# Branch B's output product: two plain tiles, then two tiles as one seven-block product, in turn

## The chip, the core and the metric

The kernel runs on one core of one Trainium2 chip, as one program. The metric is device time in microseconds. The kernel before takes 1298.48 us (median of 3 runs, 1298.05 to 1299.4). A change of this kernel is called faster or slower here when the medians differ by more than 0.2%, which is 2.6 us.

## The reference, cut to what matters

One inference step of a one-layer encoder over 576 frames (512 of a new stream, 64 of a running one), `D_MODEL = 1024`, all in float32:

```python
x = x + 0.5 * swiglu_ffn(rms_norm(x, ffn1_norm), ffn1_w_gate_up, ffn1_w_down)
h = rms_norm(x, mix_norm)
p = h @ w_in                       # seven parts of 1024 columns
...                                # branch A: a short convolution
y_a = (a_b * a_conv) @ w_a_out
...                                # branch B: a convolution of 31 taps
b_act = silu(layer_norm(b_conv + conv_b_bias, conv_b_ln_g, conv_b_ln_b))
y_b = b_act @ w_b_out
merged = sigmoid(gate_a) * y_a + sigmoid(gate_b) * y_b
x = x + merged @ w_out
x = x + 0.5 * swiglu_ffn(rms_norm(x, ffn2_norm), ffn2_w_gate_up, ffn2_w_down)
```

A final RMSNorm gives the outputs, beside the new histories of both convolutions. The change is about `b_act @ w_b_out`, a product of 576 x 1024 by 1024 x 1024.

## The kernel before

**Layout.** Features lie on the 128 partitions, frames along the free axis. An activation is eight tiles of 128 x 576 (`T = 576`, `KT = 8`), and a tile has two halves of 288 frames (`H`). The residual is the tiles `x0` to `x7` (`X[j]`), which live in on-chip memory through the whole program.

**A plain product.** Each operand is kept as a high and a low part (`hi` rounded to the matmul's input type, `lo` what is left). An output tile takes 8 steps over the contraction x 2 halves x 3 parts (hi·hi, hi·lo, lo·hi) = 48 matmuls of 128 x 288 (`mm`), into the two banks of one accumulator buffer `mm_n`. There are four such buffers, taken in turn.

**A block product.** Both feed-forward parts already compute a pair of output tiles by Winograd's form of Strassen's product: seven blocks instead of eight, each 4 contraction steps x 3 parts = 12 matmuls into one bank (`block`, `Forms`, `plan_block`). A pair takes 84 matmuls in place of 96. It needs sums of the weights (four additions of 128 x 512 tiles), sums of the activations (`combine`: four half-tile operations on each pair of tiles, then their high and low parts), and VectorE steps that put the seven results together.

**Weights.** `Stream` takes weights through three steps per unit of 128 x 512. SyncE issues the load of a `raw` tile from HBM (six raw buffers, L228, in strict order). ScalarE writes the high part and its negative (`begin`). Then GpSimd issues a DMA that adds the raw tile to the negative and so leaves the low part; for sums of weights VectorE subtracts instead. A raw buffer is free once that DMA has landed. `lead` keeps six units done ahead of the unit that TensorE multiplies, and each engine runs its instructions in the order in which the program emits them.

**Around the change.** The last two stages of the mixer go as follows. Eight plain products `p6` give gate B (`gb_of`), while `work` holds the steps of branch B's normalisation and swish, which make the operand tiles `BA[0..7]`. Then eight plain products `yb` by `w_b_out`: after each, VectorE multiplies by the gate, adds to `M[j]` (branch A's share) and, with ScalarE, splits the sum into `MS[j]`, 3.05 us of work in a chain. Then eight products `o` by `w_out`, contraction over `MS[0..7]`, whose results are added to `X[j]`. `M` had buffers of its own, four in the pool `act` and four in the pool `w`.

## Time and profile before

| | |
|---|---|
| median of 3 runs | 1298.48 us (1298.05 to 1299.4) |
| the profiled execution, device time | 1297.62 us |
| its span in the profile | 1295.8 us, so 1.82 us lie around it |
| TensorE busy | 1283.5 us, 99% of the span |
| VectorE busy | 897.0 us, 69% |
| ScalarE busy | 763.7 us, 59% |
| granted TensorE clock over the run | 0.997 |

In the profiled execution the eight `p6` products run from 748.1 to 798.0 us, the eight `yb` products to 847.9, and the `o` products follow. All of VectorE's, ScalarE's and GpSimd's instructions carry line 83 (the recording helper), so rows are told apart by their tiles. A row of the timeline gives start, duration, engine, operation and, in brackets, how long the engine sat idle before it and what ended that. Times in the windows view are busy microseconds of each engine in a stretch; its "DMA share" is how busy the core's 16 DMA engines were on average.

### The profile page before, as it was taken

How to read it: one execution, taken by the hardware profiler on the slowest of the kernel's cores; microseconds unless marked ns; L12 is line 12 of the kernel's file. 1: busy time of each engine (PE TensorE's matmuls, PEld its weight loads, DVE VectorE, ACT ScalarE, POOL GpSimd, SP SyncE). 2: the span in 40 equal slices, each digit the busy share in tenths (PEclk: the TensorE clock that was granted, in tenths of full speed). 3: DMA queues.
4: the chain of work that ended last, by engine and by line, in shares of the span. 5: the costliest groups of instructions: out<-in, count | busy, mean ns of one | idle time of the engine just before them, and what ended most of it. 6: DMA issues, size and time to landing. Idle time of an engine off the chain costs nothing.

```text
span 1295.8 us, 25664 instructions
## 1 busy us (share of the span) xinstructions
PE 1283.5 (99%) x9754; PEld 1281.9 (99%) x9754; DVE 897.0 (69%) x1480; ACT 763.7 (59%) x1351; POOL 372.0 (29%) x470
## 2 busy tenths in 40 slices
PE   9999999999999999999999999999999999999996
PEld 9999999999999999999999999999999999999996
DVE  6868668648846998898884160336867858847955
ACT  7655646546776655555544674467665656654664
POOL 0032332232333444333321322222242242241230
PEclk9999999999999999999999999999999999999998
DMA  7286786886798898877885977776697696796782
GB/s 215 74 180 153 164 179 153 175 181 151 151 194 185 168 206 175 169 168 169 178 170 117 211 158 164 169 154 139 145 179 171 145 199 149 161 206 140 159 176 80
DMA packets 285931, 213.15 MB, mean 164 GB/s; under 512 B 15344, under 2 KB 248816, under 8 KB 285808
## 3 DMA queue, kind: packets, MB, share of 16 engines
q0 software_dynamic: 57600, 95.05, 44.9%
q1 hardware_dynamic: 226336, 115.49, 31.4%
q8 instruction: 77, 1.26, 0.4%
q10 hardware_dynamic: 1872, 0.97, 0.3%
q14 instruction: 46, 0.38, 0.1%
HBM read 113.81 MB, written 2.62 MB: 90 GB/s over the span
## 4 chain that ended last, share of the span: by engine, by line
PE 96%; DVE 2%; ACT 1%; DMA 1%; issue 0%; DVEq 0%; SPq 0%; ACTq 0%
PE mm L83 96%; DVE acc L83 0%; DMA raw<-in_ffn_w_gate_up_dram 0%; ACT tmp L83 0%; DVE tmp L83 0%; DVE g L83 0%; DVE act L83 0%; DMA gains<-in_params_dram 0%; ACT act L83 0%; DVE x L83 0%; ACT g L83 0%; DVEq L1254 0%; DVE r L83 0%; ACT r L83 0%; ACT acc L83 0%
## 5 line engine op out<-in xcount | busy, mean ns | idle before, releaser
L83 PE MATMUL mm<-act,u 128*128 128x288 f32 x4686 | 659.8, 293 | 0.0
L83 PEld LDWEIGHTS mm<-act,u 128*128 128x128 f32 x4686 | 630.5, 188 | 0.0
L83 PE MATMUL mm<-act,g 128*128 128x288 f32 x2778 | 398.8, 294 | 0.1
L83 PEld LDWEIGHTS mm<-act,g 128*128 128x128 f32 x2778 | 377.5, 188 | 0.3 <-DVE tmp L83 0.3
L83 PE MATMUL mm<-act,act 128*128 128x288 f32 (+2 forms) x2244 | 306.1, 293 | 0.0
L83 PEld LDWEIGHTS mm<-act,act 128*128 128x128 f32 x2244 | 297.3, 188 | 0.0
L83 POOL DMA_DIRECT2D u<-raw x197 | 172.5, 876 | 409.9 <-ACT u L83 298.2
L83 ACT CAST u<-raw 128x512 fp32r<-128x512 f32 (+2 forms) x203 | 116.2, 572 | 156.1 <-PE mm L83 119.1
L83 POOL DMA_DIRECT2D g<-raw x117 | 102.3, 874 | 272.9 <-ACT g L83 212.7
L83 DVE SCALAR_TENSOR_TENSOR w<-g,prm,w 128x606 f32<-128x606 f32 x232 | 179.2, 842 | 1.4 <-ACT w L83 1.4
L83 DVE TENSOR_TENSOR tmp<-mm,tmp 128x288 f32<-128x288 f32 (+1 forms) x239 | 107.6, 458 | 67.8 <-PE mm L83 50.9
L83 POOL DMA_DIRECT2D act<-raw x86 | 74.7, 869 | 196.1 <-ACT act L83 187.7
L83 ACT ACTIVATE u<-u 128x512 fp32r<-128x512 f32 (+2 forms) x197 | 116.9, 593 | 6.2
L83 ACT CAST g<-raw 128x512 fp32r<-128x512 f32 (+2 forms) x126 | 69.0, 548 | 39.1 <-DMA raw<-in_ffn_w_down_dram 15.8
L83 DVE SCALAR_TENSOR_TENSOR tmp<-mm,r 128x576 f32<-128x576 f32 x48 | 36.3, 757 | 71.8 <-PE mm L83 71.8
L83 ACT CAST u<-w 128x512 fp32r<-128x512 f32 x79 | 48.9, 619 | 60.1 <-DVE w L83 52.8
L83 ACT CAST g<-w 128x512 fp32r<-128x512 f32 x77 | 47.7, 619 | 60.1 <-DVE w L83 51.5
L83 ACT CAST act<-tmp 128x576 fp32r<-128x576 f32 x84 | 56.7, 675 | 42.7 <-DVE tmp L83 41.1
L83 DVE TENSOR_TENSOR act<-tmp,act 128x576 fp32r<-128x576 f32 x84 | 62.1, 755 | 18.2 <-ACT act L83 16.5
L83 ACT ACTIVATE g<-g 128x512 fp32r<-128x512 f32 (+2 forms) x117 | 66.4, 568 | 3.7
L83 ACT CAST act<-raw 128x512 fp32r<-128x512 f32 (+3 forms) x94 | 55.6, 592 | 14.5 <-PE mm L83 6.6
L83 DVE TENSOR_TENSOR w<-raw,raw 128x512 f32<-128x512 f32 x78 | 53.4, 685 | 12.8 <-DMA raw<-in_ffn_w_gate_up_dram 12.8
(88 smaller groups left out, 808.6 us busy)
## 6 DMA issues: line engine op xcount, KB each, us to landing
raw<-in_ffn_w_gate_up_dram SPq DMA_DIRECT2D x171, 256.0 KB, 3.4
u<-raw POOLq DMA_DIRECT2D x140, 256.0 KB, 4.1
raw<-in_w_in_dram SPq DMA_DIRECT2D x112, 256.0 KB, 3.6
act<-raw POOLq DMA_DIRECT2D x80, 256.0 KB, 4.0
raw<-in_ffn_w_down_dram SPq DMA_DIRECT2D x96, 192.0 KB, 3.8
g<-raw POOLq DMA_DIRECT2D x60, 256.0 KB, 3.9
g<-raw POOLq DMA_DIRECT2D x43, 192.0 KB, 4.5
u<-raw POOLq DMA_DIRECT2D x41, 192.0 KB, 4.5
```

The costliest lines, as they stand in the source:

```text
L83: return self.tc.keep_in_program_order(fn(*args, **kwargs))
```

## The change

Of the eight `yb` tiles, tiles 0, 1, 4 and 5 stay plain products. Tiles 2 and 3, and tiles 6 and 7, become one block product each. In the program's order: plain 0, plain 1, block pair (2, 3), plain 4, plain 5, block pair (6, 7). What belongs to it:

- The block product's activation sums are formed from branch B's swish tiles: two of the four `combine`/`split` steps inside `work` during `p6`, two after the last `p6` product.
- The weights of a pair are loaded as four `raw` tiles with every second row block (`step=2`), and the units' pools are chosen by hand (`homes_b`, `few`). During `p6` four units are kept ready instead of six (`ws.ahead = 4`), and six again from `yb` on.
- `M` is now `X` itself: the residual is stored to DRAM (`kept0` to `kept7`, eight stores of 288 KB) after the first feed-forward part, branch A's share is written over it, and it is loaded back (eight loads of 288 KB, `back`) once `MS[j]` has been made. Both kinds go on SyncE's queue, among the weight loads: as built, `kept0` to `kept7` stand between the last loads of the first feed-forward part's `w_down` and the tenth load of `w_in`, each behind the last update of its `X[j]`.
- `o`'s weight units now lie in the pools `g` and `u` rather than `act` and `u`.

```diff
     for j in range(KT):
         for b, of in ((1, c_of), (2, cv_of), (0, b_of)):
             product(("p", b, j), xg, of(j))
-
-    M, SGB, BA = [], [], []
+        nc.sync.dma_start(kept[j], X[j])
+
+    M, SGB, BA = X, [], []
...
+        if i in (3, 5):
+            work.append(lambda p=(i - 3) // 2: forms.combine(p))
+        if i in (4, 6):
+            work.append(lambda p=(i - 4) // 2: forms.split(p))
+    ws.ahead = 4
...
+    for p in range(KU // 2, KU):
+        forms.combine(p)
     take()
-    MS = []
-    for j in range(KT):
-        ps = product(("yb", j), BA)
-        dve.tensor_tensor(halves(SGB[j]), ps, halves(SGB[j]), op=ALU.mult)
-        dve.tensor_tensor(M[j], M[j], SGB[j], op=ALU.add)
-        MS.append(split(M[j]))
+    for p in range(KU // 2, KU):
+        forms.split(p)
...
+    ws.ahead = AHEAD_UNITS
+    bs = forms.operands(BA[::2] + BA[1::2])
+    def merged(j, c):
+        dve.tensor_tensor(M[j], M[j], c, op=ALU.add)
+        if j < 4:
+            MS[j] = split(M[j])
+    def plain_pair(i):
+        for j in (2 * i, 2 * i + 1):
+            ps = product(("yb", j), BA)
+            dve.tensor_tensor(halves(SGB[j]), ps, halves(SGB[j]), op=ALU.mult)
+            merged(j, SGB[j])
+    def block_pair(i):
...
+        def second():
+            dve.tensor_tensor(u3, q[3], u2, op=ALU.add)
+            dve.tensor_tensor(half(c2, 1), u3, q[2], op=ALU.subtract)
+            if i == KU - 1:
+                MS[4], MS[5] = split(M[4]), split(M[5])
+        def first():
+            dve.tensor_tensor(half(c1, 1), q[5], u4, op=ALU.add)
+            dve.tensor_tensor(c1, c1, SGB[j], op=ALU.mult)
+            merged(j, c1)
...
+        for n, xs in enumerate(bs):
+            q.append(block(ws.get(plan["yb", "s", i][n]), xs))
+            if n > 0:
+                steps[n - 1]()
+        dve.tensor_tensor(half(c2, 0), q[6], u3, op=ALU.add)
+        dve.tensor_tensor(c2, c2, SGB[j + 1], op=ALU.mult)
+        merged(j + 1, c2)
+    plain_pair(0)
+    block_pair(1)
+    back(0, 1)
+    plain_pair(2)
+    back(2, 3)
+    block_pair(3)
+    MS[6], MS[7] = split(M[6]), split(M[7])
+    back(4, 5)
...
         ps = product(("o", j), MS)
+        if n == 0:
+            back(6, 7)
```

How the instructions stand now, at the three places that matter. First VectorE from the gating of `yb` tile 1 on. Before (`mm_n` are the accumulators, `w`/`g` the gate tiles, `act` the halves of the split):

```order
L83 TENSOR_TENSOR w_1585_9774<-mm_1645_10198,w_1585_9774 128x576
L83 TENSOR_TENSOR act_1440_8744<-act_1440_8744,w_1585_9774 128x576
L83 TENSOR_TENSOR act_1653_10265<-act_1440_8744,act_1652_10263 128x576
L83 TENSOR_TENSOR g_1599_9857<-mm_1654_10267,g_1599_9857 128x576
L83 TENSOR_TENSOR act_1458_8892<-act_1458_8892,g_1599_9857 128x576
```

and in the changed kernel (`mm_1678` and `mm_1685` hold results q0, q1 and q2, q3 of the first block pair, `mm_1693` q4, q5; `w_1689` is the first weight sum of the second pair, `tmp_1671`, `tmp_1672` and `tmp_1670` are the steps that join the blocks):

```order
L85 TENSOR_TENSOR x1_91<-x1_91,w_1572_9771 128x576
L85 TENSOR_TENSOR act_1668_10324<-x1_91,act_1667_10322 128x576
L85 TENSOR_TENSOR g_1666_10294<-w_1662_10262,g_1665_10293 128x512
L85 TENSOR_TENSOR tmp_1671_10328<-mm_1678_10342,tmp_1671_10328 128x288
L85 TENSOR_TENSOR tmp_1672_10329<-mm_1685_10382,tmp_1671_10328 128x288
L85 TENSOR_TENSOR w_1689_10416<-raw_1676_10338,raw_1677_10340 128x512
L85 TENSOR_TENSOR tmp_1672_10329<-mm_1685_10382,tmp_1671_10328 128x288
L85 TENSOR_TENSOR tmp_1670_10327<-tmp_1672_10329,mm_1685_10382 128x288
L85 TENSOR_TENSOR w_1694_10440<-w_1689_10416,raw_1681_10360 128x512
L85 TENSOR_TENSOR tmp_1669_10326<-mm_1693_10425,tmp_1671_10328 128x288
L85 TENSOR_TENSOR tmp_1669_10326<-mm_1693_10425,tmp_1672_10329 128x288
L85 TENSOR_TENSOR tmp_1669_10326<-tmp_1669_10326,g_1589_9859 128x576
```

Each plain tile was three operations on VectorE. Now the joining steps of the first pair stand in one row with the weight sums of the second, and `w_1689`, which reads two raw tiles, stands ahead of everything that reads q3 to q6.

Second, SyncE's queue. Before, at the tail of `w_b_out`:

```order
L228 DMA raw_1630_10068<-in_w_b_out_dram 128x4x128
L228 DMA raw_1633_10099<-in_w_b_out_dram 128x4x128
L228 DMA raw_1639_10135<-in_w_b_out_dram 128x4x128
L228 DMA raw_1642_10166<-in_w_b_out_dram 128x4x128
L228 DMA raw_1648_10204<-in_w_b_out_dram 128x4x128
L228 DMA raw_1651_10235<-in_w_b_out_dram 128x4x128
```

and now (`raw_1650` and `raw_1675` are the weights of tile 5; `raw_1676`, `raw_1677`, `raw_1681` and `raw_1684` those of the second pair, the first two of which are added in `w_1689`):

```order
L233 DMA raw_1650_10188<-in_w_b_out_dram 128x4x128
L233 DMA raw_1675_10336<-in_w_b_out_dram 128x4x128
L1163 DMA x0_90<-kept0_6553 128x576
L233 DMA raw_1676_10338<-in_w_b_out_dram 128x4x128
L1163 DMA x1_91<-kept1_6554 128x576
L233 DMA raw_1677_10340<-in_w_b_out_dram 128x4x128
L233 DMA raw_1681_10360<-in_w_b_out_dram 128x4x128
L233 DMA raw_1684_10380<-in_w_b_out_dram 128x4x128
L233 DMA raw_1688_10401<-in_w_out_dram 128x4x128
L233 DMA raw_1692_10423<-in_w_out_dram 128x4x128
L1163 DMA x2_92<-kept2_6555 128x576
L1163 DMA x3_93<-kept3_6556 128x576
```

The reloads of `x0` to `x3` stand between the weight loads, each of them behind the split of the tile that it overwrites.

Third, VectorE at the seam between `yb` and `o`. Before (tile 6's split, tile 7, the first result of `o`):

```order
L83 TENSOR_TENSOR g_1634_10125<-mm_1690_10543,g_1634_10125 128x576
L83 TENSOR_TENSOR w_1538_9467<-w_1538_9467,g_1634_10125 128x576
L83 TENSOR_TENSOR act_1698_10610<-w_1538_9467,act_1697_10608 128x576
L83 TENSOR_TENSOR g_1635_10127<-mm_1699_10612,g_1635_10127 128x576
L83 TENSOR_TENSOR w_1547_9534<-w_1547_9534,g_1635_10127 128x576
L83 TENSOR_TENSOR act_1707_10679<-w_1547_9534,act_1706_10677 128x576
L83 TENSOR_TENSOR x0_88<-mm_1710_10684,x0_88 128x576
```

and now (`x4` to `x7` are the merged tiles 4 to 7, `mm_1740` holds q4 and q5, `mm_1751` q6 of the second pair, `mm_1759` is the first `o` product):

```order
L85 TENSOR_TENSOR act_1742_10733<-x4_94,act_1741_10731 128x576
L85 TENSOR_TENSOR act_1744_10737<-x5_95,act_1743_10735 128x576
L85 TENSOR_TENSOR tmp_1717_10619<-mm_1740_10716,tmp_1719_10621 128x288
L85 TENSOR_TENSOR tmp_1717_10619<-mm_1740_10716,tmp_1720_10622 128x288
L85 TENSOR_TENSOR tmp_1717_10619<-tmp_1717_10619,g_1633_10151 128x576
L85 TENSOR_TENSOR x6_96<-x6_96,tmp_1717_10619 128x576
L85 TENSOR_TENSOR tmp_1718_10620<-mm_1751_10766,tmp_1720_10622 128x288
L85 TENSOR_TENSOR tmp_1718_10620<-tmp_1718_10620,g_1642_10173 128x576
L85 TENSOR_TENSOR x7_97<-x7_97,tmp_1718_10620 128x576
L85 TENSOR_TENSOR act_1753_10787<-x6_96,act_1752_10785 128x576
L85 TENSOR_TENSOR act_1755_10791<-x7_97,act_1754_10789 128x576
L85 TENSOR_TENSOR x0_90<-mm_1759_10799,x0_90 128x576
```

The splits of tiles 4 and 5 and both tiles of the pair now end close together, with four splits in place of one between the last blocks and the first result of `o`.

More of the change, by code (lines that the diff above doesn't have):

```diff
@@ L1 @@
+from collections.abc import Iterator
 from contextlib import ExitStack
+from itertools import cycle
 import concourse.bass as bass
@@ L204, in __init__, with raw @@
             self.sums, self.eager = {}, False
-        def raw(self, w, row0, k, col0):
-            ap = w[0, row0 : row0 + k * P, col0 : col0 + P].rearrange("(k p) n -> p k n", p=P)
-            self.raws.append((ap, k))
+        def raw(self, w, row0, k, col0, step=1):
+            rows = w[0, row0 : row0 + k * P] if step == 1 else w[0]
+            ap = rows[:, col0 : col0 + P].rearrange("(k a p) n -> a p k n", a=step, p=P)
+            self.raws.append((ap[row0 // P if step > 1 else 0], k))
             self.last.append({})
@@ L316, in plan_tile @@
             r = ws.raw(w, row0, k, col0)
-            plan[name].append(ws.unit(r, k, home_of or home(other), low))
+            to = next(home_of) if isinstance(home_of, Iterator) else home_of or home(other)
+            plan[name].append(ws.unit(r, k, to, low))
             row0 += k * P
@@ L386, in tile_encoder_step @@
         plan_mixer(("ya", j), w_a_out, j * P)
+    few = cycle(("u", "u", "u", "act"))
     for j in range(KT):
-        plan_mixer(("p", 6, j), w_in, 6 * D + j * P)
-    for j in range(KT):
-        plan_mixer(("yb", j), w_b_out, j * P)
+        plan_mixer(("p", 6, j), w_in, 6 * D + j * P, few)
+    homes_b = iter((
+        "u", "act", "u", "act", "u", "act", "u", "act", "u", "g", "act",
+        "u", "act", "u", "g", "u", "act", "u", "g", "u", "act", "g",
+    ))
+    for i in range(KU):
+        pair = 2 * i, 2 * i + 1
+        if i % 2 == 0:
+            for j in pair:
+                plan_mixer(("yb", j), w_b_out, j * P, homes_b)
+        else:
+            plan_block(("yb", "s", i), [
+                ws.raw(w_b_out, h * P, KU, j * P, 2) for j in pair[::-1] for h in range(2)
+            ], [next(homes_b) for _ in range(7)])
     for j in IN_TURN:
-        plan_mixer(("o", j), w_out, j * P)
+        plan_tile(("o", j), w_out, 0, (KU, KU), j * P, "g")
     plan_ffn("f2", ffn2_gu, ffn2_dn)
@@ L1022, in b_of @@
         return then
+    kept = [
+        dram.tile([P, T], F32, tag=f"kept{j}", name=f"kept{j}") for j in range(KT)
+    ]
     for j in range(KT):
@@ L1051, in swish @@
             BA[j] = (BA[j], low(sig[j], BA[j]))
+            forms.b.setdefault(j // 2, []).append(sig[j])
     def ga_of(j):
@@ L1060, in then @@
         def then(ps):
[L1061 to L1063 removed]
+            dve.tensor_tensor(halves(M[j]), ps, halves(gates.pop(j)), op=ALU.mult)
         return then
@@ L1103, in tile_encoder_step @@
         advance()
-    work.extend((lambda i=i: swish(i, RL)) for i in range(KT + 2))
+    for i in range(KT + 2):
+        work.append(lambda i=i: swish(i, RL))
+        if i in (3, 5):
[3 more added lines that the diff above has]
+    ws.ahead = 4
     def gb_of(j):
@@ L1118, in tile_encoder_step, with back @@
         work.pop(0)()
+    for p in range(KU // 2, KU):
+        forms.combine(p)
     take()
-    MS = []
-    for j in range(KT):
-        ps = product(("yb", j), BA)
-        dve.tensor_tensor(halves(SGB[j]), ps, halves(SGB[j]), op=ALU.mult)
-        dve.tensor_tensor(M[j], M[j], SGB[j], op=ALU.add)
-        MS.append(split(M[j]))
+    for p in range(KU // 2, KU):
+        forms.split(p)
+    MS = [None] * KT
+    def back(*js):
+        for j in js:
+            nc.sync.dma_start(X[j], kept[j])
@@ new lines, in tile_encoder_step @@
+    ws.ahead = AHEAD_UNITS
[10 more added lines that the diff above has]
+    def block_pair(i):
+        j = 2 * i
+        c1, c2, qu, uu = (ttile() for _ in range(4))
+        q1, u2, u3, u4 = half(qu, 0), half(qu, 1), half(uu, 0), half(uu, 1)
+        q = []
+        def second():
[7 more added lines that the diff above has]
+            merged(j, c1)
+        steps = (
+            lambda: sca.copy(q1, q[0]),
+            lambda: dve.tensor_tensor(u2, q[1], q1, op=ALU.subtract),
+            lambda: dve.tensor_tensor(u4, q[2], u2, op=ALU.subtract),
+            second,
+            lambda: dve.tensor_tensor(half(c1, 0), q[4], q1, op=ALU.add),
+            first,
+        )
+        for n, xs in enumerate(bs):
[5 more added lines that the diff above has]
+        merged(j + 1, c2)
+        spare.clear()
@@ L1128, in tile_encoder_step @@
+    plain_pair(0)
[6 more added lines that the diff above has]
+    back(4, 5)
+    ss = Sum()
+    xg = [None] * KT
+    forms = Forms(R_N2)
     ss = Sum()
```

11 lines of the change are left out of this document (5 added, 6 removed).

## The prediction

> **What bounds the kernel now.** I read the page's first part, then what TensorE (PE) waited for, then the chain of waits.
>
> ```profile
> span 1295.8 us, 25664 instructions
> PE 1283.5 (99%) x9754; PEld 1281.9 (99%) x9754; DVE 897.0 (69%) x1480; ACT 763.7 (59%) x1351; POOL 372.0 (29%) x470
> ...
> PE mm L83 <- DVE acc L83: 1.5, 1, 1.5
> PE mm L83 <- POOL eps L83: 1.0, 1, 1.0
> PE mm L83 <- DVE tmp L83: 0.4, 1, 0.4
> ...
> 25.94 1246.14 PE mm L83 x9490
> ```
>
> Busy PE alone would prove little, since matmuls overlap. But its waits come to 2.9 us in all, and the chain runs through 9490 matmuls without a break from 25.94 us to 1272.08. So between those times a matmul fewer is worth its full spacing, and any wait that reaches PE costs its full length. The stretches around the change, and one at the end of the first feed-forward part:
>
> ```profile
> core 0: us, PE busy (x) PEld busy (x) DVE busy (x) ACT busy (x) POOL busy (x), PEclk, DMA share, GB/s
> 375.00:400.00 25.00, 25.00 (x192) 25.00 (x191) 12.65 (x17) 18.03 (x32) 9.03 (x11) 1.00 1.00 200
> 750.00:775.00 25.00, 25.00 (x195) 25.00 (x194) 19.97 (x31) 22.37 (x36) 6.49 (x9) 1.00 0.72 150
> 775.00:801.00 26.00, 26.00 (x202) 26.00 (x201) 0.00 (x0) 12.14 (x21) 6.74 (x8) 1.00 0.88 182
> 801.00:826.00 25.00, 25.00 (x194) 25.00 (x193) 9.07 (x12) 10.34 (x19) 6.03 (x7) 1.00 0.74 157
> 826.00:851.00 25.00, 25.00 (x195) 25.00 (x194) 9.12 (x13) 11.94 (x20) 6.90 (x8) 1.00 0.78 167
> ```
>
> PE is full at clock 1.00 in each; VectorE (DVE) does nothing from 775 to 801 us and a third of the `yb` stage; ScalarE (ACT) is nearly full from 750 to 775 only.
>
> **The gain.** Per pair of tiles 96 matmuls become 84, for two pairs 24 fewer. Their spacing is read from starts, plain ones in `yb` (first and last of eight rows) and blocks in the second feed-forward part (first and last of 26):
>
> ```profile
> 804.06 3.28 PE L83 MATMUL mm<-act,act 128*128 128x288 f32 x24
> 825.90 3.28 PE L83 MATMUL mm<-act,u 128*128 128x288 f32 x24
> ...
> 1001.13 1.74 PE L83 MATMUL mm<-act,u 128*128 128x288 f32 x12
> 1040.83 1.76 PE L83 MATMUL mm<-act,g 128*128 128x288 f32 x12
> ```
>
> Plain: 21.84 us over 7 steps, 3.12 us per 24 matmuls, 0.130 us each. Blocks: 39.70 us over 25 steps, 1.588 us per 12, 0.132 us each. So a block's matmul is not free of overhead: a plain pair takes 4 x 3.12 = 12.48 us, a block pair 7 x 1.588 = 11.12 us. The change removes 2 x 1.36 = **2.73 us**, not 24 x 0.130 = 3.12 us.
>
> The Trainium skill ("TensorE: Matmul & The Clock Gate", section "Wait — 56ns, not 53.3ns?") gives a warm matmul N/2.4 ns plus a fixed 2.5 ns, 122.5 ns at 288 columns, whatever product it belongs to. By that (an estimate) the change would remove 24 x 0.1225 = 2.94 us; both measured spacings are longer than its figure, and they differ from each other.
>
> **Sums of the activations.** 16 half-tile operations and 8 low parts on DVE, 8 casts on ACT. Durations from the same forms:
>
> ```profile
> L83 DVE TENSOR_TENSOR tmp<-mm,tmp 128x288 f32<-128x288 f32 x16 | 7.1, 451 | 1.8 <-ACT tmp L83 1.8
> L83 DVE TENSOR_TENSOR w<-raw,raw 128x512 f32<-128x512 f32 x6 | 4.1, 685 | 0.0
> L83 ACT CAST act<-tmp 128x576 fp32r<-128x576 f32 x8 | 5.4, 670 | 1.7 <-DVE tmp L83 1.5
> L83 DVE TENSOR_TENSOR act<-tmp,act 128x576 fp32r<-128x576 f32 x8 | 6.0, 752 | 1.6 <-ACT act L83 1.6
> ```
>
> That is 16 x 0.45 + 8 x 0.75 = 13.2 us of DVE and 8 x 0.67 = 5.4 us of ACT. What hides it is PE's own `p6` stage: DVE idles for 26 us from 775 on, ACT for 14 of them, and PE reads `BA` first at 798 (the gating of tile 0 starts at 804.26, one product of 6.24 later). The sums are needed only with the first pair, 12.5 us after that. In the order ACT now also waits, ahead of swish, for buffers that PE releases halfway through `p6`'s first product, about 3 us; the spare covers that too. Price nothing; uncovered, 13.2 us.
>
> **The stores of `X`.** Eight of 288 KB, on SP's queue among loads of 256 KB. No row shows one. By bytes they cost as the loads do:
>
> ```profile
> DMA packets 20973, 16.61 MB, mean 163 GB/s; under 512 B 1004, under 2 KB 16897, under 8 KB 20962
> q1 hardware_dynamic: 16392, 8.14, 27.5%
> ...
> u<-raw POOLq DMA_DIRECT2D x16, 256.0 KB, 3.9
> raw<-in_w_b_out_dram SPq DMA_DIRECT2D x16, 256.0 KB, 3.1
> act<-raw POOLq DMA_DIRECT2D x15, 256.0 KB, 3.7
> ...
> act<-raw POOLq DMA_DIRECT2D x20, 256.0 KB, 4.8
> u<-raw POOLq DMA_DIRECT2D x20, 256.0 KB, 5.4
> ```
>
> This is the DMA view of 748 to 850 us, and in the last two rows that of 380 to 500 us. 27.5% of 102 us for 8.14 MB is 3.45 us of all 16 engines per MB, so 1.0 us for a tile and 8.1 us for the eight stores. They fall about 370 to 400 us, where the share is already 1.00. Bounds: 0 (the weights are ahead) and 8.1 us (no lead). I take 0: the weights run six units ahead, 6 x 18 matmuls x 0.130 = 14 us, against some 7 us from a unit's cast to its landed low part. A gain is excluded, since PE had no wait there. The eight reloads cost 8.1 us of engine time more in a stage with a share of 0.74 to 0.78, spread over 45 us: 0.18 more, nothing alone, but it can lengthen landings.
>
> **The joints: where a wait could arise.** This is the step that decides. In the order, the first weight sum of the second pair (`w_1689`) needs `raw_1677`, whose buffer was the last unit of the first pair's. Its way, by steps of the kernel before:
>
> ```profile
> 810.50 0.76 DVE L83 TENSOR_TENSOR w<-mm,w 128x576 f32<-128x576 f32 x1 [3.19 <-PE mm L83]
> 811.29 0.76 DVE L83 TENSOR_TENSOR act<-act,w 128x576 f32<-128x576 f32 x1
> 812.79 0.76 DVE L83 TENSOR_TENSOR act<-act,act 128x576 fp32r<-128x576 f32 x1 [0.74 <-ACT act L83]
> ...
> 805.84 0.68 ACT L83 CAST act<-act 128x576 fp32r<-128x576 f32 x1 [4.83 <-DVE act L83]
> 806.42 0.62 ACT L83 CAST act<-raw 128x512 fp32r<-128x512 f32 x1
> 807.07 0.63 ACT L83 ACTIVATE act<-act 128x512 fp32r<-128x512 f32 x1
> ...
> 808.00 0.86 POOL L83 DMA_DIRECT2D act<-raw  x1 [5.83 <-ACT act L83]
> ...
> 812.76 0.37 SPq L228 DMA_DIRECT2D raw<-in_w_b_out_dram  x1
> ...
> DMA to landing us min/median/max: 3.3/3.6/4.7
> ```
>
> The last row is for the low parts landing in `act` from 800 to 850 us. Let 0 be the end of tile 1 on PE (810.48 in the trace of before). Gate and add end at 1.6, the high part of tile 1 at 2.2 as before, the unit's cast starts there, POOL issues 1.58 later (806.42 to 808.00) at 3.75, and SP can load the buffer again 4.76 after that (808.00 to 812.76), at 8.5. The load lands 3.1 later, at 11.7, and `w_1689` ends at 12.4. PE has left the block pair at 11.1 and multiplies tiles 4 and 5 until 11.12 + 12.48 = 23.6, the second pair until 34.7.
>
> Behind `w_1689` on DVE wait the joining steps of q3 to q6 and the sums of the second pair. Up to the third sum stand 5 half-tile operations, 3 of 512 and 6 of 576 columns and two stops of 0.74 for ACT's high parts: 2.25 + 2.06 + 4.56 + 1.48 = 10.35 us end to end, so 22.75; rows that do not read each other start up to 0.08 before the last ends, which makes it 22.3. Then ACT casts the sum and prepares a12 (0.62 + 1.26), POOL and the landing take 0.3 + 4.76: 29.2 to 29.7. PE wants that low part at 23.6 + 4 x 1.588 + 0.26 = 30.2, so 0.5 to 1.0 us is spare. The same sum for a22, 3.6 us of DVE later, gives 32.4 to 33.3 against 33.4: 0.1 to 1.0 us spare.
>
> Behind that ACT goes on without a stop: four unit preparations of 1.2, a copy, two high parts. DVE then has the low parts of tiles 4 and 5, and 5 us in one row (q4, q5, the gate, tile 6, q6, tile 7) to the low part of tile 6. End to end it is ready at 39.45 to 40.9. The first `o` product starts at 34.7 and reads it in its seventh step: 34.7 + 36 x 0.130 + 0.13 = 39.5. So PE waits 0 to 1.4 us there; tile 7's low part comes 0.7 later, with PE 0.78 later. Queued behind the wait is everything of PE. Against the upper end stands a row of the page: in the feed-forward parts the same weight sum waits for its load, and PE, by its waits above, waits for nothing in all 39 block pairs (two such sums to a pair):
>
> ```profile
> L83 DVE TENSOR_TENSOR w<-raw,raw 128x512 f32<-128x512 f32 x78 | 53.4, 685 | 12.8 <-DMA raw<-in_ffn_w_gate_up_dram 12.8
> ```
>
> That row is nearest, so I take **0.4 us**, near the lower end. All three waits share their slack: a wait at the earlier one gives the later one time.
>
> **Sum.** -2.73 + 0.4 = -2.3 us. The profiled execution took 1297.62 us (span 1295.8, 1.82 around it), so it would become 1295.3 us. The median of the runs is 0.86 us above it: **1296.1 us**, 0.18% less. A change of this kernel can be told from none beyond 0.2%, 2.6 us, so below 1295.9 or above 1301.1.
>
> **Rivals.**
> - *Every matmul costs the same, no wait* (0.22). -3.12 us, 1295.4 us, just on the faster side. For it: the matmuls are the same instructions. Against it: the 25 steps of 1.588 us.
> - *The joints hold PE* (0.20). If `raw_1677` lands 1 us late (4.7 against 3.6 is the worst landing in the stage) and DVE runs end to end, the low part of tile 6 is 1.4 + 1 late: -2.73 + 2.4, 1298.2 us. For it: six low parts are issued within 9 us, where before two came per 6.24, and tiles of `x` share the queue.
> - *Slower: the stores hold up the weights* (0.06). One place, 375 to 400 us, with a DMA share of 1.00. If the 8.1 us of the stores become a delay of the loads behind them on SP and the lead covers none of it, PE pays 8.1 us: 1298.48 + 8.1 - 2.73 = 1303.9. It decides from the point where loads come more than the 7 us late that the lead leaves. Against it: the share falls to 0.72 to 0.88 later, where backlog is worked off. The Trainium skill ("DMA: Bandwidth & Descriptors", section "Issuing engines are not separate DMA queues") says that transfers of all issuing engines run on the same 16 DMA engines and interleave. By that rule the stores also slow POOL's low parts, and the trace agrees: from 380 to 500 us, under the higher share, these land in 4.8 to 5.4 us, against 3.7 to 3.9 above.
> - *The change doesn't do what it says* is excluded as far as the count goes: the built program has 24 matmuls fewer.
>
> **Numbers.** My forecast has 0.52, its own range 1295.5 to 1296.9, and about a third of it lies beyond 0.2% when the wait at the joint is nearly nothing. Faster: 0.22 + 0.18 = 0.40. Slower: 0.06. The same: the rest of the forecast, 0.34, and the joints, 0.20, so 0.54. The range 1295.0 to 1298.4 takes in all but the slower case and late landings beyond the bound.
>
> **What would show it.** The `yb` stage, from the first row of tile 0 to the first of `o`, lasts 4 x 6.24 + 2 x 11.12 = 47.2 us instead of 49.9. PE's waits between 30 and 1270 us show one of a few tenths on an `act` tile of DVE, at the first `o` product; an idle DVE ahead of `w<-raw,raw`, ended by a load of `w_b_out`, comes just before tile 4. No wait at 375 to 420 us. Wrong would be: a wait inside the block pairs for POOL's low parts, blocks at 1.56 us, or a longer stage before 748 us.

## The result, and the profile after

The changed kernel takes 1301.72 us (median of 9 runs, 1298.68 to 1303.84), the kernel before, beside it on the same chip, 1298.25 us (1297.94 to 1299.4). The ratio is 1.0026, 95% interval 1.0018 to 1.0035: 3.5 us slower. The forecast was 2.3 us faster, and its range ended at 1298.4. So the sign was wrong. The one rival on the slower side (stores that hold up the weights) did not happen either.

The profiled execution took 1301.72 us, span 1299.9, against 1295.8 before. Two lines of the page and TensorE's (PE's) own waits:

```profile
span 1299.9 us, 25738 instructions
PE 1284.2 (99%) x9730; PEld 1281.0 (99%) x9730; DVE 924.0 (71%) x1534; ACT 770.8 (59%) x1365; POOL 369.7 (28%) x468
...
PE mm L85 <- ACT act L85: 1.6, 1, 1.6
...
PE mm L85 <- DMA g<-raw: 0.9, 1, 0.9
PE mm L85 <- DVE act L85: 0.4, 1, 0.4
...
PE mm L85 <- DMA u<-raw: 0.3, 1, 0.3
```

There are 24 matmuls fewer, yet PE is busy 0.7 us longer. These four waits, 3.2 us, are new; the three left out (`acc`, `eps`, `tmp`) are those of before. The stretches of the prediction, and the one behind them:

```profile
core 0: us, PE busy (x) PEld busy (x) DVE busy (x) ACT busy (x) POOL busy (x), PEclk, DMA share, GB/s
375.00:400.00 25.00, 25.00 (x192) 25.00 (x192) 11.89 (x17) 19.22 (x33) 10.16 (x12) 1.00 1.05 245
...
775.00:801.00 26.00, 26.00 (x202) 26.00 (x201) 12.01 (x22) 19.34 (x33) 8.60 (x10) 1.00 0.94 202
...
826.00:851.00 25.00, 24.08 (x181) 23.65 (x180) 19.53 (x34) 14.54 (x25) 6.88 (x8) 1.00 0.74 162
851.00:876.00 25.00, 23.05 (x173) 22.60 (x172) 11.19 (x19) 18.41 (x30) 6.02 (x7) 1.00 1.06 258
```

PE is full where the stores are (375 to 400 us, DMA share 1.05) and where the activations' sums are made (775 to 801, where DVE now works 12 us). It has holes only from 826 us on. The timeline of PE shows them place by place:

```profile
811.56 1.74 PE L85 MATMUL mm<-act,u 128*128 128x288 f32 x12
...
822.67 3.33 PE L85 MATMUL mm<-act,u 128*128 128x288 f32 x24
...
835.32 1.74 PE L85 MATMUL mm<-act,u 128*128 128x288 f32 x12
...
846.41 4.78 PE L85 MATMUL mm<-act,g 128*128 128x288 f32 x34 [0.92 <-DMA g<-raw]
851.03 1.75 PE L85 MATMUL mm<-act,u 128*128 128x288 f32 x12
854.32 0.40 PE L85 MATMUL mm<-act,u 128*128 128x288 f32 x1 [1.55 <-ACT act L85]
855.12 1.72 PE L85 MATMUL mm<-act,u 128*128 128x288 f32 x11 [0.39 <-DVE act L85]
856.67 3.32 PE L85 MATMUL mm<-act,g 128*128 128x288 f32 x24
```

The first block pair takes 11.11 us, as forecast. Tiles 4 and 5 take 12.65, 0.17 more. The 24 matmuls of `o` in the row at 846.41 run at 3.16 us, so `o` starts at 851.03 - 3.16 = 847.87, and the second block pair took 12.55 instead of 11.12. The first `o` product then takes 8.80 us (to 856.67) instead of 6.24. So `yb` is 1.6 us longer than forecast (0.17 + 1.43), and 2.6 us more went at the first `o` product.

### The profile page after: what moved, and what is told of

The parts are those of the page before. It is cut to its first block, busy times and chain, and to the rows that moved or that the text cites. A ratio compares the mean times of both kernels' runs of the same rounds, so it can differ in the third digit from the quotient of the medians.

```text
span 1299.9 us, 25738 instructions
## 1 busy us (share of the span) xinstructions
PE 1284.2 (99%) x9730; PEld 1281.0 (99%) x9730; DVE 924.0 (71%) x1534; ACT 770.8 (59%) x1365; POOL 369.7 (28%) x468
## 4 chain that ended last, share of the span: by engine, by line
PE 76%; issue 12%; DMA 4%; DVE 3%; POOL 2%; ACT 2%; POOLq 0%; DVEq 0%; SPq 0%; ACTq 0%
PE mm L85 76%; POOL u L85 1%; DMA raw<-in_w_b_out_dram 1%; DMA u<-raw 1%; POOL act L85 1%; DMA act<-raw 1%; DVE tmp L85 1%; DMA raw<-in_w_out_dram 0%; ACT u L85 0%; DMA raw<-in_w_in_dram 0%; DVE acc L85 0%; ACT tmp L85 0%; DVE act L85 0%; ACT act L85 0%; DVE x L85 0%
## 5 line engine op out<-in xcount | busy, mean ns | idle before, releaser
L85 PE MATMUL mm<-act,u 128*128 128x288 f32 x4758 | 670.8, 294 | 2.3 <-ACT act L85 1.6
L85 PEld LDWEIGHTS mm<-act,u 128*128 128x128 f32 x4758 | 640.8, 188 | 3.1 <-ACT act L85 1.8
L85 PE MATMUL mm<-act,g 128*128 128x288 f32 x3030 | 434.7, 294 | 1.0 <-DMA g<-raw 0.9
L85 PEld LDWEIGHTS mm<-act,g 128*128 128x128 f32 x3030 | 412.0, 188 | 1.5 <-DMA g<-raw 1.2
L85 PE MATMUL mm<-act,act 128*128 128x288 f32 (+2 forms) x1896 | 259.5, 293 | 0.0
L85 PEld LDWEIGHTS mm<-act,act 128*128 128x128 f32 x1896 | 251.6, 188 | 0.3 <-DVE act L85 0.2
L85 POOL DMA_DIRECT2D g<-raw x127 | 110.7, 871 | 302.3 <-ACT g L85 249.4
L85 POOL DMA_DIRECT2D act<-raw x70 | 60.8, 868 | 115.3 <-ACT act L85 106.2
L85 ACT ACTIVATE g<-g 128x512 fp32r<-128x512 f32 (+2 forms) x127 | 72.8, 573 | 4.0
L85 ACT ACTIVATE tmp<-tmp 128x576 f32<-128x576 f32 x47 | 32.2, 685 | 46.0 <-DVE tmp L85 46.0
```

Of the source, the lines that this page charges most:

```text
L85: return self.tc.keep_in_program_order(fn(*args, **kwargs))
```

## Three theories of the waits

What feeds these waits is the joint that the prediction described. On SP, DVE and ACT it went like this (three views of the changed kernel):

```profile
819.33 0.37 SPq L233 DMA_DIRECT2D raw<-in_w_b_out_dram  x1
```

```profile
825.95 0.69 DVE L85 TENSOR_TENSOR w<-raw,raw 128x512 f32<-128x512 f32 x1 [7.40 <-DMA raw<-in_w_b_out_dram]
...
854.30 1.43 DVE L85 TENSOR_TENSOR act<-x,act 128x576 fp32r<-128x576 f32 x2 [1.28 <-ACT act L85]
```

```profile
852.43 0.62 ACT L85 CAST u<-raw 128x512 fp32r<-128x512 f32 x1 [3.23 <-DMA raw<-in_w_out_dram]
...
853.62 1.23 ACT L85 CAST act<-x 128x576 fp32r<-128x576 f32 x2
```

`raw_1677` was issued at 819.33, 7.8 us after PE had gone on from tile 1 to the block pair (811.56; the forecast's 8.5 counts from 0.2 us later), and landed 6.6 us later (forecast 3.1). At the seam to `o`, ACT stood 3.23 us at the cast of a weight unit of the third `o` product, whose load had not landed. The casts of tiles 6 and 7 stand behind it, DVE's low parts behind those (854.30), and PE's next matmul behind these (854.32).

- **Theory 1: the buffer comes free late**, because its last unit (a22) is cast behind tile 1's split.
- **Theory 2: the landing is long**, because reloads of `x` and low parts share the 16 DMA engines with it.
- **Theory 3: ACT's order at the seam decides**: tiles 6 and 7 stand behind a weight unit that is late.

Two further questions came from the traces: the spacing of plain matmuls, and stretches of matmuls at half speed.

## The experiments

**a22 earlier.** ACT casts a22 ahead of tile 1's split:

```diff
             ps = product(("yb", j), BA)
+            if j % 2:
+                ws.lead(plan["yb", "s", i + 1][0])
             dve.tensor_tensor(halves(SGB[j]), ps, halves(SGB[j]), op=ALU.mult)
```

> One part of the joint is moved: the last unit of the first block pair (a22) is cast on ACT ahead of the split of tile 1 and not behind it, so its raw buffer should come free about 3.4 us earlier. Theory 1 (the buffer comes late): the load of raw_1677 is issued about 3.4 us earlier, DVE's idle time ahead of the sum that reads it falls from 7.4 us to about 4, PE's waits inside the second block pair (1.3 us) go and those at the first o product fall from about 2.4 to 1 us: about 2 to 3 us faster than the changed kernel (1301.7), so 1298.7 to 1299.7. Theory 2 (the landing is long, 6.5 us instead of 3.1, because reloads of x and low parts share the 16 DMA engines): the load is still long, the sum gains under 1 us, and the time stays within 0.8 us of the changed kernel. Theory 3 (ACT's order at the seam decides): the waits inside the block pair go, that at the first o product stays at 2 us: 1300.4.

Measured: 1298.09 us against 1297.72 before, ratio 1.0003 (0.9994 to 1.0012). The sum, and PE's waits apart from those at the ends:

```profile
817.72 0.69 DVE L85 TENSOR_TENSOR w<-raw,raw 128x512 f32<-128x512 f32 x1 [0.77 <-DMA raw<-in_w_b_out_dram]
...
PE mm L85 <- DVE act L85: 0.4, 1, 0.4
PE mm L85 <- DMA u<-raw: 0.3, 1, 0.3
```

DVE's stop fell from 7.40 to 0.77 us, the waits inside the block pair are gone, and those at the first `o` product fell to 0.9 us. By the medians this one order of two casts is worth about the 0.2% that the change had lost, as theory 1 said. Of the 6.6 us by which DVE's stop shrank, 3.6 come from the earlier issue (4.2 us after tile 1 instead of 7.8) and 3.0 from a landing of 3.6 us instead of 6.6. The first part is the edit's: in all six traces of kernels with this edit, those below included, the stop is 0.7 to 1.8 us, and in the five traces with the old order it is 4.9 to 7.4. What is left at the seam speaks for theory 3 as well.

**Reloads later, a miss.** The calls that load `x` back were moved behind the first `o` product in the source:

```diff
     block_pair(1)
-    back(0, 1)
...
         if n == 0:
-            back(6, 7)
+            back(*IN_TURN)
```

> All eight reloads of x are issued behind the first o product, none inside the yb stage; nothing else differs. Theory 1 (the buffer comes late): raw_1677 is issued at the same place and lands at most 1 us earlier; time within 0.8 us of the changed kernel (1301.7). Theory 2 (the reloads share the DMA engines with it): it lands 3 to 3.6 us after issue instead of 6.5, the sum comes 3 us earlier, and 2 to 3 us of PE's waits go: 1298.7 to 1299.7. Theory 3 (ACT's order at the seam): wait at the first o product stays at about 2 us.

Measured: 1299.67 us against 1297.72, 1.0020 (1.0009 to 1.0030). The trace shows the reloads where they had been (`x0` at 807.37, `x1` at 813.54): SP's transfers are not kept in the order of the source, and the program is the changed kernel again. So it told nothing of theory 2, but is a second measurement of the change. In it `raw_1677`, issued at 818.13, landed by 822.24, in 4.1 us and not 6.6, so that length changes from run to run, and PE had no wait inside the second block pair.

**The lead cut at the seam.**

```diff
         for n, xs in enumerate(bs):
+            if i == KU - 1 and n > 3:
+                ws.ahead = 10 - n
...
     MS[6], MS[7] = split(M[6]), split(M[7])
+    ws.ahead = AHEAD_UNITS
```

> Only the seam is changed: in the last block pair the lead over the units of o is cut to four units, so ACT casts the high parts of tiles 6 and 7 ahead of the fifth and sixth unit of o and not behind them. Theory 3 (the cast of tile 6 stands behind a weight unit whose load is late): PE's wait at the first o product falls from about 2.4 us to under 0.8, waits inside the block pair stay at 1.3 us: about 1.6 us faster than the changed kernel, 1300.1. Theories 1 and 2 (the late sum pushes all of DVE's work of the pair): the split of tile 6 is late on DVE anyway and the wait stays at 1.5 us or more: within 0.8 us of the changed kernel. If the units of o become late instead, a new wait appears at the third o product.

Measured: 1299.41 us against 1297.72, 1.0015 (1.0006 to 1.0024).

```profile
853.74 1.76 PE L85 MATMUL mm<-act,u 128*128 128x288 f32 x11 [1.03 <-DVE act L85]
```

The wait at the first `o` product fell from 1.55 + 0.39 to 1.03 us, and its releaser is no longer ACT but DVE, which is late for theory 1's reason; the wait inside the second block pair stayed (0.76 us). So the wait lies between what theory 3 (under 0.8) and theory 1 (1.5 or more) had said, and both hold a part. `raw_1677` landed in 6.5 us here. New waits (0.3 and 0.4 us) came behind `o`. Against the 1299.67 of the second measurement of the change the median shows no gain.

**One block pair alone**, tiles 6 and 7 or tiles 2 and 3. In the plan and in the sequence the other pair is plain again (the diff is that of the first kernel; with its homes, and the splits of tiles 4 to 7 in the second kernel, as a plain pair has them):

```diff
-        if i % 2 == 0:
+        if i != 3:
             for j in pair:
...
-    block_pair(1)
+    plain_pair(1)
```

> Only tiles 6 and 7 are a block pair; tiles 2 and 3 are plain again, so 12 matmuls fewer than before and not 24, and no unit of an earlier block holds a raw buffer. Theories 1 and 2 (the late sum of the second block pair): DVE has no idle time ahead of that sum that reaches PE, no wait inside the pair, under 0.8 us at the first o product: -1.36 + 0.6 for o at 131.7 ns + 0.4 = about 0.4 us faster than before (1298.3), 3.8 faster than the changed kernel. Theory 3 (the order at the seam): the wait at the first o product stays near 2 us, so about 1.2 us slower than before. Apart from that every run here tells by its first 70 us whether the 1.4 us that the changed kernel lost there (plain products of the first feed-forward part at 134.4 ns a matmul instead of 130.0) go with the program or change from run to run.

> Only tiles 2 and 3 are a block pair; tiles 4 to 7 are plain, so there is neither a late sum of a second block pair nor a block at the seam to o. By the terms measured so far: -1.36 us for the pair, +1.67 ns for each of the 576 plain matmuls behind it if these stay at 131.7 ns (0.96 us), and 0.3 to 1.0 us at the first block pair of the second feed-forward part: between 0.4 us faster and 0.6 us slower than before, no wait over 0.3 us in yb and none at the first o product, and no half-rate stretch. If a wait of a us or more stays at the first o product, it isn't the block there that makes it.

Measured: tiles 6 and 7 alone 1297.47 us against 1297.72, 1.0001 (0.9992 to 1.0010). Tiles 2 and 3 alone 1297.65 against 1298.04, 0.9997 (0.9988 to 1.0006). In the first kernel PE waits neither in `yb` nor at the first `o` product, and ACT stops for no load at the seam. Its order there is that of the changed kernel, so by itself the order of theory 3 costs nothing: it costs when a load that stands in it is late. In the second kernel PE has no new wait at all. From tile 4 to the last `o` product its plain matmuls take 3.16 us per 24. Two rows of it, then two of `o` in the first kernel:

```profile
824.76 3.32 PE L85 MATMUL mm<-act,act 128*128 128x288 f32 x24
827.92 3.32 PE L85 MATMUL mm<-act,u 128*128 128x288 f32 x24
```

```profile
862.67 3.39 PE L85 MATMUL mm<-act,u 128*128 128x288 f32 x24
865.89 3.39 PE L85 MATMUL mm<-act,g 128*128 128x288 f32 x24
```

-1.36 for a pair and 576 x 1.67 ns = +0.96 make -0.40; from the first `yb` row to the end of `o` the trace has -0.32 against before. Here the sum closes. In the first kernel the same instructions of `o` run at 3.23 us, 134.4 ns each: -1.36 and 384 x 4.4 ns = +1.69 make +0.33, and the trace has +0.47. So **the plain matmuls behind a block pair are slower** in these traces, 131.7 or 134.4 ns where those ahead of it ran at 130.0, and most of a pair's gain, or all of it, goes there.

**Dummies.** 54 matmuls that nobody reads, on top of the earlier a22:

```diff
+    def dummy(n, v):
+        t = psum2()
+        for _ in range(n):
+            pe.matmul(t[:, 0, :H], ones_r, v[:, :H], start=True, stop=True)
```

> Adds 54 matmuls whose result nobody reads (288 columns, ones as weights), in groups of 1 to 7: ahead of the third and sixth down product of groups 1 to 3 in the first feed-forward part (1, 2, 3 each time) and in the second (4, 5, 6), one ahead of tile 4 and 4 and 7 ahead of the third and sixth o product; otherwise the kernel with a22 earlier. 54 x 0.130 = 7 us longer by themselves. It tells what sets the spacing of plain matmuls (130.0, 131.7 or 134.4 ns). Theory A (a state of PE's sequence that any interruption of the six-matmul pattern sets anew): the spacing behind a group of dummies differs from that ahead of it in at least a third of the places. Theory B (it belongs to the product: which buffers its weights and activations lie in): the spacing of each product stays as in the kernel without them. Theory C (the four matmuls with ones of a mean are what resets it): only the groups of 4 return it to 130.0.

Measured: 1304.09 us, one run; 54 x 0.130 = 7.0 over the 1297.1 of the profiled kernel with a22 earlier. What stands behind a group of two (164.48 us, its own row first) and behind one of four:

```profile
164.48 0.44 PE L85 MATMUL mm<-act,ones_r 128*128 128x288 f32 x2
164.75 2.50 PE L85 MATMUL mm<-act,g 128*128 128x288 f32 x18
167.09 1.72 PE L85 MATMUL mm<-act,u 128*128 128x288 f32 x12
...
965.50 2.58 PE L85 MATMUL mm<-act,g 128*128 128x288 f32 x18
967.92 1.78 PE L85 MATMUL mm<-act,u 128*128 128x288 f32 x12
```

Behind the two, 18 take 2.34 us, 130.0 ns each; behind the four, 18 take 2.42, 134.4 each; ahead of both they ran at 131.7. But only 4 of the 15 groups changed the spacing: one of the two groups of two, two of the three of four, one of the two of five. So the spacing does not belong to the product alone and an interruption can set it anew (B falls), the four matmuls of a mean are not a sure reset (C falls), and A, which expected a third of the places, is right in kind and too strong in number. What sets the spacing stays open.

**Both kernels once more**, unchanged, for second traces.

> The changed kernel once more, unchanged, for a second trace. If the spacing of matmuls is set anew in each execution, the first plain products of the first feed-forward part run at 130.0 or 131.7 ns and not at 134.4 as in the first trace, or tiles 4 and 5 and o run at another spacing than 131.7. If it goes with the program, both are as before. The load of raw_1677 lands 6 to 7 us after its issue again if that is the program's doing, and near 3 us if it was chance.

> The kernel before once more, unchanged. If the spacing is set anew in each execution, its first plain products run at another spacing than the 130.0 ns of its first trace; if it goes with the program, they run at 130.0 again. No wait in the yb stage, and none at the first block pair of the second feed-forward part (a low part there lands 3.6 us after its issue, just when PE comes to it), unless that landing changes from run to run.

Measured: 1300.87 us and 1297.9 us. The first plain products of the first feed-forward part, first and last of four rows, in the first trace of before and in that of the change:

```profile
29.17 3.28 PE L83 MATMUL mm<-act,u 128*128 128x288 f32 x24
38.53 3.28 PE L83 MATMUL mm<-act,g 128*128 128x288 f32 x24
```

```profile
29.47 3.39 PE L85 MATMUL mm<-act,u 128*128 128x288 f32 x24
39.15 3.39 PE L85 MATMUL mm<-act,g 128*128 128x288 f32 x24
```

9.36 and 9.68 us for 72 matmuls: 130.0 and 134.4 ns. In the second trace of before it was 131.7, in the second of the change too, and 130.0 in that of the kernel with the moved calls, which is the same program. So the spacing there changes between executions of one program, and the 1.3 us that the changed kernel's first trace lost before `yb` are no cost of the change. The second trace of before has no wait in `yb` or at the block pairs, and in that of the change `raw_1677` landed in 4.2 us. Behind the blocks, tiles 4 and 5 and `o` ran at 131.7 in both traces of the change: that part goes with the program. And the second trace showed something else, PE's rows at the first `o` product and two stretches of 3.41 us:

```profile
851.56 0.40 PE L85 MATMUL mm<-act,u 128*128 128x288 f32 x1 [1.40 <-ACT act L85]
...
854.03 4.77 PE L85 MATMUL mm<-act,g 128*128 128x288 f32 x24
858.64 3.32 PE L85 MATMUL mm<-act,u 128*128 128x288 f32 x24
```

```profile
850.38:853.79 3.41, 1.83 (x11) 1.62 (x12) 1.43 (x2) 3.38 (x6) 0.86 (x1) 1.00 1.11 300
853.79:857.21 3.42, 3.42 (x17) 3.42 (x16) 1.33 (x2) 3.36 (x7) 1.72 (x2) 0.50 1.12 302
```

The 24 matmuls from 854.03 take 4.61 us instead of 3.16. For 3.41 us the granted clock was 0.50, with the matmuls 240 ns apart (17 in it, where the stretch behind it has 28). The wait of 1.40 us cost 1.5 us more after it was over.

**The price of a wait.** Eight waits put into the kernel before, between 505 and 670 us:

```diff
+    def stall(n, v):
+        p, q, h = psum2(), psum2(), ttile()
+        pe.matmul(p[:, 0, :H], ones_r, v[:, :H], start=True, stop=True)
+        sca.copy(half(h, 0), p[:, 0, :H])
+        for i in range(n):
+            pool.tensor_copy(half(h, (i + 1) % 2), half(h, i % 2))
+        pe.matmul(q[:, 0, :32], ones, half(h, n % 2)[:, :32], start=True, stop=True)
```

> The kernel before with eight waits put into its three-projection stage (560 to 690 us): PE is made to wait for a chain of a copy on ACT and 1, 2, 1, 2, 1, 2, 3 and 0 copies on POOL behind its own last matmul. It computes the same. It measures the price of a wait on PE by itself. Theory A (a wait costs its length and 0.1 us): each place costs its gap, and the spacing behind it is 130.0 to 134.5 ns. Theory B (after enough idle time in a stretch of a few us TensorE's clock is halved): behind waits above about 1.7 us, not all of them, some 14 matmuls follow at 240 ns, 1.5 us more; behind waits under 1 us none do. The spacing after a wait without such a stretch tells, besides, whether a wait sets the spacing of plain matmuls anew.

Measured: 1330.26 us, one run. The second wait on PE, then the windows of it and of what follows, and that of the third wait:

```profile
528.74 0.41 PE L83 MATMUL mm<-tmp,ones 128*128 128x32 f32 x2 [1.91 <-POOL tmp L83]
528.98 4.96 PE L83 MATMUL mm<-act,act 128*128 128x288 f32 x24
```

```profile
526.26:529.67 3.41, 1.50 (x12) 1.27 (x11) 3.41 (x5) 2.74 (x6) 2.28 (x5) 1.00 0.26 77
529.67:533.09 3.42, 3.42 (x16) 3.42 (x15) 2.70 (x4) 1.62 (x3) 2.25 (x3) 0.50 0.73 123
...
550.15:553.56 3.41, 2.65 (x20) 2.65 (x21) 3.34 (x6) 3.35 (x7) 2.04 (x4) 1.00 0.26 61
```

The waits of 1.91, 2.00, 2.36, 2.55 and 5.86 us were each followed by such a stretch (6.8 us at the longest), those of 0.49, 1.04 and 1.05 by none. Theory B holds. Besides, the plain matmuls behind the first wait ran at 131.7 or 134.4 ns, and no longer at the 130.0 of before, up to the mean behind that stage (749 us).

The windows lie on one grid through an execution: from the stretch at 853.79 us above to the drop of the clock at that program's end (1290.70 us) are 128.0 lengths of 3.413 us. On this grid, in all 16 traces and from 10 us on, every window at full clock in which PE was busy 1.84 us or less was followed by half clock, and none with 1.85 us or more was. Near that edge lie 1.74 and 1.83 us on the one side, 1.85, 1.86 and eight windows of 1.89 or 1.90 on the other.

The Trainium skill ("TensorE: Matmul & The Clock Gate", section "What's actually happening") says that the clock is halved after an idle window of about 3.4 us, in windows that run free of the program. The length of the stretches, 3.41 us, and the fixed grid agree; that the window must be idle doesn't: PE was busy 1.83 of 3.41 us in the one that triggered it above.

**Two `o` products interleaved**, on top of the earlier a22, so that PE meets tiles 6 and 7 later:

```diff
+        if n == 0:
+            first2 = both([("o", i) for i in IN_TURN[:2]], MS)
-        ps = product(("o", j), MS)
+        ps = first2[n] if n < 2 else product(("o", j), MS)
```

> On top of the earlier a22 the first two products of o are interleaved term by term, as the first two down products of the feed-forward parts are, so that PE reads tiles 6 and 7 4.7 us later. Theory 3 (the split of tiles 6 and 7 stands at the end of ACT's and DVE's queues and PE meets it): the waits of about 1 us at the first o product go to 0, and the median falls by 0.7 to 1.0 us against the kernel with a22 earlier alone (1298.1), to about 1297.2. If instead the unit preparations for four o units at once become late, the wait only changes its name (a low part of o) and the time stays.

Measured: 1300.70 us against 1298.17, 1.0020 (1.0011 to 1.0029), by the ratios 2.2 us slower than the kernel with a22 earlier, where 0.7 to 1.0 us faster was expected.

```profile
849.39 6.83 PE L85 MATMUL mm<-act,g 128*128 128x288 f32 x38 [2.73 <-DMA g<-raw]
```

The wait for tiles 6 and 7 did go. But the second product's weights are now wanted 24 matmuls earlier, and PE waited 2.73 us for a low part, at once followed by 14 matmuls at 240 ns: the wait changed its name, and grew past the edge.

**Tiles 4 and 5 split earlier**, with the earlier a22, without and with the moved calls of the reloads, and with the lead cut:

```diff
+        def early():
+            dve.tensor_tensor(u4, q[2], u2, op=ALU.subtract)
+            if i == KU - 1:
+                MS[4], MS[5] = split(M[4]), split(M[5])
...
-            lambda: dve.tensor_tensor(u4, q[2], u2, op=ALU.subtract),
+            early,
```

> The kernel with a22 earlier; besides, in the last block pair the splits of tiles 4 and 5 come one step earlier, so ACT casts their high parts ahead of one more weight unit of o (1.2 us) and DVE, which stood still 2.0 us for them, reaches the joins of tiles 6 and 7 about 1.2 us sooner. If ACT's and DVE's order at the seam is what PE still meets there, the waits of 1.0 us at the first o product go to 0 to 0.2 us and the median falls by 0.7 to 1.0 us against 1298.1, to 1297.2. If the load of the weight unit behind which the cast of tile 6 stands is what is late, ACT waits for that load 1.2 us longer, and nothing changes. No long wait is left, so no execution should have a stretch of matmuls at 240 ns there, and the runs should spread by 2 to 3 us and not by 5.

> The same, and all reloads of x behind the first o product. If the reloads still lengthen landings that PE or ACT meets, this is faster than the kernel without it by 0.2 us or more; if they only mattered while raw_1677 was late, the two are within 0.2 us of each other, or this one is slower because x arrives late for the sums of the first o products.

> All three edits at the seam together: a22 earlier, the splits of tiles 4 and 5 one step earlier, and the lead over the units of o cut to four in the last block pair, so that no weight unit whose load is late stands ahead of the casts of tiles 6 and 7 on ACT. If that cast is all that is left of the wait at the first o product (0.5 and 0.66 us with the two edits alone), it goes: 1.0 us less than 1297.2, about 1296.2 us, 0.14% below the kernel before. If the units of o then come late, as some waits behind 905 us did in the kernel with the lead alone cut, waits of 0.3 to 1 us appear at later o products or at the start of the second feed-forward part, and the time stays near 1297.2. No half-rate stretch in either case, since no window of 3.4 us has 1.7 us of waiting.

Measured: 1297.17 us against 1298.03, 0.9995 (0.9986 to 1.0004). With the moved calls 1298.44, 1.0000 (0.9991 to 1.0009); this is again the same program as the one without them, so the two together tell that medians of one such program differ by 1.3 us, and that the 1 us under the kernel with a22 earlier is not shown. With the lead cut too 1297.91 against 1298.08, 0.9998 (0.9989 to 1.0007). In this last kernel the first `o` product has no wait (its last 24 matmuls are the first row):

```profile
848.57 3.41 PE L85 MATMUL mm<-act,u 128*128 128x288 f32 x24
...
902.92 0.66 PE L85 MATMUL mm<-tmp,ones_r 128*128 128x288 f32 x3 [0.40 <-DVE tmp L85]
```

From the first `yb` row to the end of `o` it gained 2.26 us on before, nearly the forecast. Some 0.5 us of that is luck: at 861 us the spacing in `o` went back to 130.0 ns without a wait, as it did at 865 us in the kernel with the lead alone cut. PE then came to the mean behind `o` before DVE had its sum (0.40 us in the second row, 1.0 with the gaps around it), and to the first block pairs of the second feed-forward part before their weights: 2.0 us were given back. No kernel here is shown to be faster than before.

**Reloads on ACT's queue**, the real test of theory 2:

```diff
-            nc.sync.dma_start(X[j], kept[j])
+            sca.dma_start(X[j], kept[j])
```

(with the calls behind the first `o` product, as above).

> The reloads of x are issued by ACT behind the first o product and not by SP inside the yb stage; this time they do move (the earlier edit left SP's order as it was, since the scheduler places those transfers by itself, so that kernel was the changed kernel once more). Everything else is the changed kernel. Theory 2 (the reloads share the DMA engines with the load of raw_1677): issued at the same place, some 9 us behind the start of the first block pair, it lands 3.0 to 3.6 us later and not 4.1 to 6.5, the sum that reads it starts 0.5 to 3 us earlier, and the median is 0.7 to 2 us under the changed kernel's (1.0020 and 1.0026 of before), so 0.05 to 0.1% above before. Theory 1 (only the buffer that comes free late counts): landing and time as in the changed kernel, 0.2% above before. New at the end of the stage: x0 and x4 come only behind the first o product, which DVE can wait for without PE.

Measured: 1305.75 us against 1298.04, 1.0061 (1.0048 to 1.0074). Views of SP, DVE and ACT:

```profile
818.43 0.37 SPq L233 DMA_DIRECT2D raw<-in_w_b_out_dram  x1
```

```profile
822.96 0.69 DVE L85 TENSOR_TENSOR w<-raw,raw 128x512 f32<-128x512 f32 x1 [4.87 <-DMA raw<-in_w_b_out_dram]
```

```profile
867.38 0.78 ACT L85 ACTIVATE act<-x,gains 128x576 fp32r<-128x576 f32 x1 [10.93 <-DMA x<-kept]
```

No reload ran in `yb` now, and the load still took 4.5 us, not the 3.0 to 3.6 of theory 2; with them it took 6.6, 6.5, 4.2 and 4.1 in the four traces with the same order up to there, and 3.6 in that of the earlier a22. So the reloads are not what keeps it above 3.6. Whether they have a part in the 6.5, one trace without them can't tell, and the low parts' share in theory 2 was not tested. The time tells nothing of theory 2, since the kernel has a new cost: ACT's queue issued the eight transfers between 855.83 and 867.34 us, the fifth and the sixth 6.9 us apart, and ACT's next instruction came after 10.93 us. PE had new waits for ACT at the end of `o` (1.79 us the longest) with one stretch at half clock; that these go back to ACT's stop is inferred, and why the sixth issue came so late is open.

## Why the prediction was wrong

- ***Gain*, -2.73 us: right.** Block pairs of 11.11 us, and -0.32 where -0.40 was the sum with one pair and no joint.
- ***Sums of the activations* and *stores*, price 0: right.** No wait from 375 to 420 us at a DMA share of 1.05, none in `p6` with DVE busy 12 us in the idle stretch.
- ***The joints*, 0.4 us: this step failed.** In the first trace they cost 1.4 us inside the second block pair and 2.5 at the first `o` product. Two of its assumptions broke. One was the landing of `raw_1677`, 3.1 forecast, 4.1 to 6.6 measured; with 0.1 to 1.0 us of slack at the low parts, the 6.6 of the first trace was by itself enough for the wait inside the pair. Where it took 4.1 or 4.2, issued 0.9 us earlier than forecast, that wait was absent. The other was the sentence that behind the sums "ACT goes on without a stop": it stopped 3.23 us for a load of `w_out` in front of tile 6. Such a stop (2.65 us) cost 1.9 us even in the second measurement of the change, where `raw_1677` landed when the forecast had it (within 0.3 us of the 11.7 behind tile 1's end; its terms, 8.5 and 3.1, make 11.6). The row that was to hold against the upper end, 39 pairs of the feed-forward parts without a wait, does not carry over. There, too, the high part of an output tile is cast between weight units (`act<-tmp` at 939.17 us in the trace of before), but PE takes those tiles only in the down products behind a whole group of pairs, while the first `o` product reads tile 6 at once. That this is the difference is argued from the order, not tested.
- **Left out: the plain matmuls behind a block.** The prediction took 0.130 us for them, from rows of `yb` before, where no block comes ahead. Rows of before with a block ahead show 3.16 us per 24:

```profile
1047.17 3.32 PE L83 MATMUL mm<-act,g 128*128 128x288 f32 x24
1050.33 2.54 PE L83 MATMUL mm<-act,u 128*128 128x288 f32 x18
```

  480 matmuls (tiles 4 and 5, `o`) at 1.67 ns more are 0.80 us, a third of the gain. It could have been read.
- **Left out: what a wait costs afterwards.** Beyond its length, 1.5 us at half clock once some 1.6 us of a 3.41 us window are waiting. The change sits on that edge: PE was busy 1.86 us of the worst window in its first trace, without such a stretch, and 1.83 in the second, with one.

```profile
851.01:854.42 3.41, 1.86 (x15) 1.62 (x13) 2.06 (x5) 1.96 (x4) 0.42 (x1) 1.00 1.12 243
```

  One stretch takes 0.0013 off the mean clock. It was 0.996 or 0.997 in the 33 runs of before beside the first four experiments, and 0.994 or 0.995 in four of nine of the change (1301.4 to 1303.8 us). That fits the spread of the change's times (5.2 us against 1.5); the link in the runs without a trace is an inference.
- **Left out: the first block pair of the second feed-forward part.** PE waited there 0.2 to 0.9 us for a low part in nine of the eleven traces with two block pairs, where it landed 4.0 to 5.2 us after its issue. In the two of before it landed in 3.3 and 3.6 us, in time, and in the other two (the dummies and the reloads on ACT's queue) in 3.4. Why it lands later is open.
- **The rivals.** "The joints hold PE" named the place and the mechanism, and gave 2.4 us where the joints came to 1.9 to 3.9. Its time, 1298.2, was still too low, by the last three points. "Every matmul costs the same" was wrong: there are four spacings.

The sum from the first `yb` row to the end of the profiled execution: -2.73, joints 1.4 + 2.5, spacing 0.17 + 0.6, the second feed-forward part 0.5, together 2.4; the trace shows 2.7 up to the last matmul. Of the rest of the 4.1, 1.3 us is the chance spacing at the start.

## What to carry to other kernels

In a kernel whose PE is full, price a saved matmul together with the joint that it creates: list, for each in-order engine, what stands ahead of the cast that PE needs next, and give every load ahead of it its worst landing of the stage, not its median. A weight unit that is needed later and may be late must not stand ahead of an operand that is needed now; swapping two casts (a22 and tile 1's split) was worth nearly all that this change had lost against the kernel before, though not the gain that was hoped for. And keep the waits in any 3.4 us window well under half of it, since above that PE pays them almost twice.

## What the runs showed of the hardware that was not expected

- Plain matmuls of one shape run at 130.0, 131.7 or 134.4 ns. Behind the block pairs of `yb` they ran at 131.7 or 134.4, ahead of them at 130.0; waits and a few odd matmuls in between can set it anew, and in `o` it changed twice with neither. In the first 70 us it differs between executions of one program. The cause is open.
- A stretch of 3.41 us at half clock follows a window of the same length in which PE was busy 1.84 us or less; 1.85, 1.86 and 2.65 were enough to avoid it.
- The landing of one and the same load took 4.1, 4.2 and 6.6 us in three executions of one program, and 6.5 in one of a program that is the same up to there.
- Behind eight transfers issued from ACT's queue, ACT's own work stood still for 10.93 us.
